# Regrouping TensorE's small products in a hybrid attention and linear-attention layer

## The chip, the cores and the metric

One core of one Trainium2 chip runs the whole layer. The metric is the device time of one execution in microseconds; less is better. The engines have short names in the profile: PE is TensorE (PEld its weight loads), DVE is VectorE, ACT is ScalarE, POOL is GpSimd and SP is SyncE, which issues most of the transfers.

## What is computed

One layer of an encoder over 512 tokens of width 2048, all in float32:

```python
h = rmsnorm(x, attn_norm_w);  proj = h @ w_in
aq, ak, av, gq, gk, gv, gr, glr = split(proj)
# group A: 16 heads x 64, three dilated windows merged by their softmax denominators
attn = mixture_of_dilations(aq, ak, av, rel_bias_table)
# group B: 4 heads, dk = 128, dv = 256, gated linear attention in both directions
o = gla_causal(q, k, v, log_a_f) + flip(gla_causal(flip(q), flip(k), flip(v), flip(log_a_b)))
gla_out = rmsnorm_per_head(o) * gla_norm_w * silu(gr)
x = x + concat(attn, gla_out) @ w_out
h = rmsnorm(x, ffn_norm_w)
x = x + (silu(h @ w_gate) * (h @ w_up)) @ w_down
out = rmsnorm(x, final_norm_w)
```

With a sequence of 512 the three windows become one dense 512x512 attention with a bias (a count of the windows that hold a key goes into it). Linear attention works in four blocks of 128 tokens: scores inside a block, masked for each direction, and a running state from block to block.

## The kernel before

The order of all instructions is written out by hand. The big matrix products are *jobs*: a job multiplies one 512-wide stretch of a weight matrix, in 16 *halves* of 12 matmuls. Each float32 operand is split into a high and a low part in a reduced format (a copy by ScalarE, L196, and a subtraction by VectorE, L197, three halves ahead), and three products of parts replace one float32 product; those are lines L285 to L287 and L293 to L295. A job holds four of the eight PSUM banks until its evacuation at the end.

Between two halves (15 times per job) `run_job` lets *side work* advance: `run_side` takes one step, up to the next `yield`, of the generator at the front of the queue `side`, after one step of an `urgent` generator if there is one. Side work has the other four PSUM banks. A slot, in PSUM or SBUF, goes back to a first-in first-out list when the program has issued its last reader. In order, the jobs are: attention's q/k and v projections (`job_qk`, `job_av`), two pairs of linear attention's q/k and v, two for the output gate (`evac_gr`, whose SiLU needs another function table on ScalarE), four for the output projection. The feed-forward part follows.

*Attention.* `attention(g)` makes one `att_step(h, b)` per yield: head h, block b of 128 queries, which is a *unit*. A step issues the unit's two score products (L553, L554). Then it transposes the softmax weights of the unit before it (`att_transpose`, four transposes, L514) and, in every second step, multiplies two units' transposed weights with v (`att_av`, eight matmuls, L522 and L523). For its own unit it reads the scores (VectorE, L566), takes the exponential (ScalarE, L584) and scales (`att_norm`, VectorE, L507 and L508). The transposed weights are split into a high part (ScalarE, L578) and a low part (VectorE, L579). `att_mix` (L532, L534) writes v's products away; after the second half of an odd head it splits the finished pair of heads (`split_of`, L355 and L356).

*Linear attention.* `gla(h)` handles one head in 17 steps. After gates and decays (ScalarE and VectorE, up to L768), the products come in these steps: for each direction the scores (L782) and the transposes of k (L786); for each direction three products for the states (L810), with scaled copies by ScalarE (L818) and sums (L820); for each pair of blocks the outputs (L841), their squares (L844) and, after one normalization (L312 to L318, L854), two groups of four transposes (L860), each followed by the scaling L863 and `gla_out`. These products are plain float32; the profile records each as two matmuls. `tables` loads a function table (L149) when another one is wanted.

Nothing in `tables`, `run_side`, `run_job` or the jobs is changed.

Of the kernel before, what the change touches and what calls it, by code (L numbers as in the profile page):

```python
# [15 lines left out]
F32 = mybir.dt.float32  # L16
F32R = mybir.dt.float32r
U32 = mybir.dt.uint32
AF = mybir.ActivationFunctionType
OP = mybir.AluOpType  # L20
# [3 lines left out]
P = 128  # L24
# [87 lines left out]
def put(*slots):  # L112
    for s in slots:
        if s.home is not None:
            s.home.free.append(s.i)


def layer(nc, tc, x, attn_norm_w, w_in, rel_table, gw_f, gb_f, gw_b, gb_b, gla_norm_w, w_out,
# [4 lines left out]
    pe, act, dve, pool, sp = nc.tensor, nc.scalar, nc.vector, nc.gpsimd, nc.sync  # L123
    mm = pe.matmul

    with tc.manual_schedule(), \
# [5 lines left out]
        s2 = Slots(p2, N2, 512, "a")  # L132
        s4 = Slots(p4, N4, 1024, "b")
# [293 lines left out]
        def load_bias(h):  # L427
            if h < NH and h not in biast:
                biast[h] = s4.get(F32, [P, BIASW])
                src = bass.AP(tensor=line.tensor, offset=line.offset + h * LINE, ap=[[1, P], [1, BIASW]])  # L430
                sp.dma_start(out=biast[h].t, in_=src)
# [65 lines left out]
                side.append(attention(2 * half))  # L497
            return f

        at = {"prev": None, "av": None, "u": 0}  # L500
        am = [small[:, 56 + i:57 + i] for i in range(4)]
        asum = [small[:, 60 + i:61 + i] for i in range(4)]
        ar = [small[:, 64 + i:65 + i] for i in range(4)]
# [6 lines left out]
        def att_transpose(u):  # L510
            h, b, n, L = u[:4]
            t = ps.get()
            for kb in range(4):
                pe.transpose(t.t[:, kb * P:(kb + 1) * P], L.t[:, kb * P:(kb + 1) * P], idn)  # L514
            put(L)
            return t
# [25 lines left out]

        def att_step(h, b):

            cur, prev, av = None, at["prev"], at["av"]
            if h is not None:
                q, k, kl = (x_[h % 2] for x_ in QK[h // 2])
                c = slice(b * P, (b + 1) * P)
                if b == 0:
                    load_bias(h)  # L550
                    load_bias(h + 1)
                s = ps.get()
                mm(s.t, q.t[:, c], k.t, start=True, stop=False)  # L553
                mm(s.t, q.t[:, c], kl.t, start=False, stop=True)  # L554
                if b == 3:
                    put(q, k, kl)
                n = at["u"]
                at["u"] += 1
            tp = att_transpose(prev) if prev else None
            if av:  # L560
                at["av"] = None
                o = att_av(*av)
            if h is not None:
                L = s2.get()
                w = biast[h].t[:, 384 - b * P:896 - b * P]
                dve.tensor_tensor_reduce(L.t, s.t, w, 1.0, 3e38, op0=OP.add, op1=OP.min,  # L566
                                         accum_out=am[n % 4])
                put(s)
                if b == 3:
                    put(biast.pop(h))  # L570
            if prev:
                ph, pb = prev[:2]
                if pb % 2 == 0:
                    at["pt"] = (s4.get(F32R, [P, 4, 256]), s4.get(F32R, [P, 4, 256]))
                pth, ptl = at["pt"]
                cc = slice((pb % 2) * P, (pb % 2 + 1) * P)
                src = tp.t.rearrange("p (k c) -> p k c", c=P)
                act.copy(pth.t[:, :, cc], src)  # L578
                dve.tensor_tensor(ptl.t[:, :, cc], src, pth.f[:, :, cc], op=OP.subtract)  # L579
                put(tp)  # L580
                if pb % 2 == 1:
                    at["av"] = (ph, pb // 2, pth, ptl)
            if h is not None:
                act.activation(L.t, L.t, AF.Exp, scale=-1.0, bias=am[n % 4], accum_out=asum[n % 4])  # L584
                cur = (h, b, n, L)
            if av:
                att_mix(av[0], av[1], o)
            if h is not None:
                att_norm(cur)
            at["prev"] = cur  # L590

        def attention(g):
            for h in range(4 * g, 4 * g + 4):
# [106 lines left out]
        def gla_out(i):  # L700
            if i in gate and i in gout:
                t, o = gate.pop(i), gout.pop(i)
                dve.tensor_tensor(o.t, o.t, t.t, op=OP.mult)
                put(t)
                mixf[8 + i] = o
                if not hT:
                    mixh[8 + i] = split_of(mixf.pop(8 + i), big=True)
# [7 lines left out]
        def gla(h):  # L715
# [26 lines left out]
            for d in range(2):  # L742
                c = fb[d]
# [19 lines left out]
                q, k = s2.get(), s2.get()  # L763
# [11 lines left out]
                put(*G["res"])  # L775

            T, kt = [], []
            for d in range(2):
                a = ps.get()
                for b in range(4):  # L780
                    c = slice(b * P, (b + 1) * P)
                    mm(a.t[:, c], ks[d].t[:, c], qs[d].t[:, c], start=True, stop=True)  # L782
                tr = ps.get()
                for b in range(4):
                    c = slice(b * P, (b + 1) * P)
                    pe.transpose(tr.t[:, c], ks[d].t[:, c], idn)  # L786
                put(ks[d])
                t = s2.get()
                pool.memset(t.t, 0.0)
                yield  # L790
                dve.copy_predicated(r3(t), masks[:, d:d + 1, :].to_broadcast([P, 4, P]),
                                    a.t.rearrange("p (b c) -> p b c", c=P))
                put(a)
                T.append(t)
                kk = s2.get()
                act.copy(kk.t, tr.t)
                put(tr)
                kt.append(kk)
            dve.tensor_tensor(T[0].t, T[0].t, T[1].t, op=OP.add)
            put(T[1])  # L800
            yield

            v = [gv[h // 2][b // 2].t[:, b % 2, (h % 2) * 256:(h % 2 + 1) * 256] for b in range(4)]
            S_ = [{}, {}]
            for d in range(2):
                order = ((0, 1, 2), (3, 2, 1))[d]
                stt = s4.get(F32, [P, 4, 256])
                us = [ps.get() for _ in range(2)]
                for n, b in enumerate(order):
                    mm(us[n // 2].t[:, (n % 2) * 256:(n % 2 + 1) * 256], kt[d].t[:, b * P:(b + 1) * P], v[b],  # L810
                       start=True, stop=True)
                put(kt[d])
                prev = None
                for n, b in enumerate(order):
                    u = us[n // 2].t[:, (n % 2) * 256:(n % 2 + 1) * 256]
                    s = stt.t[:, n]
                    fi = fs[d][:, (b if d == 0 else b - 1):(b if d == 0 else b - 1) + 1]
                    act.activation(s, u, AF.Copy, scale=fi)  # L818
                    if prev is not None:
                        dve.scalar_tensor_tensor(s, prev, fi, s, op0=OP.mult, op1=OP.add)  # L820
                    prev = s
                    S_[d][b + 1 if d == 0 else b - 1] = s
                put(*us)
                S_[d]["slots"] = stt
                yield

            on = s4.get(F32, [P, 4, 256])
            ss, rs = small[:, 76:80], small[:, 80:84]
# [2 lines left out]
            for i in range(2):  # L831
                o = ps.get()
                for b in (2 * i, 2 * i + 1):
                    c = slice(b * P, (b + 1) * P)
                    ob = o.t[:, (b % 2) * 256:(b % 2 + 1) * 256]
                    terms = [(T[0].t[:, c], v[b])]
                    for d in range(2):
                        if b in S_[d]:
                            terms.append((qs[d].t[:, c], S_[d][b]))
                    for n, (l, r) in enumerate(terms):  # L840
                        mm(ob, l, r, start=n == 0, stop=n == len(terms) - 1)  # L841
                for b in (2 * i, 2 * i + 1):
                    ob = o.t[:, (b % 2) * 256:(b % 2 + 1) * 256]
                    act.activation(junk.t[:, 0:256], ob, AF.Square, accum_out=ss[:, b:b + 1])  # L844
                os_.append(o)
                yield
            put(junk, T[0], *qs, S_[0]["slots"], S_[1]["slots"])
            if h % 2:
                put(*gv.pop(h // 2))
            rstd_of(ss, 4, rs, 1.0 / 256, (small[:, 84:88], small[:, 88:92]))  # L850
            for i in range(2):
                for b in (2 * i, 2 * i + 1):
                    c = slice((b % 2) * 256, (b % 2 + 1) * 256)
# [3 lines left out]
            for i in range(2):  # L857
                tr = ps.get()
                for b in range(4):
                    pe.transpose(tr.t[:, b * P:(b + 1) * P],  # L860
                                 on.t[:, b, i * P:(i + 1) * P], idn)
                o = s2.get()
                dve.tensor_scalar(o.t, tr.t, wcol[:, W_GLA + 2 * h + i:W_GLA + 2 * h + i + 1], None, op0=OP.mult)  # L863
                put(tr)
                gout[2 * h + i] = o
                gla_out(2 * h + i)
                yield
            put(on)


# [734 lines left out]
```

## Time and profile before

| | |
|---|---|
| median of 3 runs | 2232.04 us (2231.92 to 2236.86) |
| profiled execution | 2234.08 us, its span 2232.3 us |
| busy share of the span | TensorE 99%, VectorE 73%, ScalarE 45%, GpSimd 5% |
| linear attention's last product | 711 us |
| output projection, then feed-forward | from 681 us, from 869 us |

The span runs from the first to the last instruction of the profiled execution. The duration of a matmul's record reaches beyond the start of the next one, because matmuls are pipelined, so a row's duration is not the time that TensorE gives to it. The distance from one start to the next is.

### The profile page before, as it was taken

The page shows a single profiled execution, that of the slowest core. Times are in us where ns is not written, and L with a number is a line of the kernel's source. Part 1 is how long each engine was busy: PE and PEld are TensorE (multiplying, and loading weights), DVE is VectorE, ACT ScalarE, POOL GpSimd, SP SyncE. Part 2 cuts the span into 40 slices and gives each one's busy share as a digit, 9 for nine tenths or more (in the row PEclk, how much of TensorE's full clock was granted, in tenths as well). Part 3 has the DMA queues.
Part 4 walks back from the last instruction along what each step waited for, and adds up shares of the span by engine and source line. Part 5 has one row for each costly group of instructions (what it writes and reads, how often), then busy time and mean ns, then how long its engine had stood idle before and what let it go on. Part 6 is the DMA issues. An engine that isn't in the chain of part 4 may idle for free.

```text
span 2232.3 us, 37013 instructions
## 1 busy us (share of the span) xinstructions
PE 2207.0 (99%) x14814; PEld 2034.4 (91%) x14814; DVE 1635.4 (73%) x2717; ACT 1002.7 (45%) x1637; POOL 116.2 (5%) x173
## 2 busy tenths in 40 slices
PE   8999999999999999999999999999999999999998
PEld 6888888888888888999999999999999999999986
DVE  4366665745454436988888888888888788988877
ACT  5344454444454344444434343444334565555543
POOL 0000000000000100000000000000000110022220
PEclk9999999999999999999999999999999999999999
DMA  6525625232314332333333333333333774588992
GB/s 206 158 68 154 177 79 147 85 123 64 97 57 151 128 127 76 113 115 124 114 114 123 114 123 114 114 125 115 122 120 116 247 179 171 185 198 184 237 372 80
DMA packets 211804, 307.78 MB, mean 138 GB/s; under 512 B 15375, under 2 KB 131263, under 8 KB 211632
## 3 DMA queue, kind: packets, MB, share of 16 engines
q1 hardware_dynamic: 192480, 259.37, 36.1%
q0 software_dynamic: 18256, 44.99, 8.5%
q8 instruction: 116, 1.90, 0.3%
q10 hardware_dynamic: 896, 1.06, 0.1%
q14 instruction: 56, 0.46, 0.1%
HBM read 246.58 MB, written 46.20 MB: 131 GB/s over the span
## 4 chain that ended last, share of the span: by engine, by line
PE 94%; DVE 2%; DMA 2%; ACT 1%; issue 0%; SPq 0%; ACTq 0%; DVEq 0%
PE ps L1149 13%; PE ps L1148 13%; PE ps L1147 13%; PE ps L293 6%; PE ps L294 6%; PE ps L295 6%; PE ps L285 5%; PE ps L287 5%; PE ps L286 5%; PE ps L1376 5%; PE ps L1375 5%; PE ps L1374 5%; PE ps L514 1%; PE ps L841 1%; DMA a<-md 1%; DMA b<-gd 1%
## 5 line engine op out<-in xcount | busy, mean ns | idle before, releaser
L1149 PE MATMUL ps<-a,b 128*128 128x256 f32 x2464 | 697.7, 283 | 2.9 <-DVE b L1106 2.9
L1147 PE MATMUL ps<-a,b 128*128 128x256 f32 x2464 | 697.4, 283 | 0.0
L1148 PE MATMUL ps<-a,b 128*128 128x256 f32 x2464 | 697.3, 283 | 0.0
L1101 ACT CAST b<-b 128x768 fp32r<-128x768 f32 x480 | 445.8, 942 | 533.4 <-DVE b L1106 285.9
L1106 DVE TENSOR_TENSOR b<-b,b 128x768 fp32r<-128x768 f32 x480 | 510.3, 1089 | 132.8 <-PE ps L1148 61.8
L1149 PEld LDWEIGHTS ps<-a,b 128*128 128x128 f32 x2464 | 473.0, 192 | 3.8 <-DVE b L1106 3.8
L1148 PEld LDWEIGHTS ps<-a,b 128*128 128x128 f32 x2464 | 473.0, 192 | 0.0
L1147 PEld LDWEIGHTS ps<-a,b 128*128 128x128 f32 x2464 | 473.0, 192 | 0.0
L197 DVE TENSOR_TENSOR a<-b,a 128x512 fp32r<-128x512 f32 x292 | 195.0, 686 | 126.9 <-ACT a L196 125.7
L1376 PE MATMUL ps<-b,a 128*128 128x256 f32 x896 | 253.7, 283 | 2.7 <-DVE a L1339 2.7
L1375 PE MATMUL ps<-b,a 128*128 128x256 f32 x896 | 253.6, 283 | 0.0
L1374 PE MATMUL ps<-b,a 128*128 128x256 f32 x896 | 253.6, 283 | 0.0
L196 ACT CAST a<-b 128x512 fp32r<-128x512 f32 x292 | 171.1, 617 | 55.8 <-DMA b<-in_w_down_dram 20.9
L293 PE MATMUL ps<-a,a 128*128 128x512 f32 x464 | 183.5, 396 | 0.0
L294 PE MATMUL ps<-a,a 128*128 128x512 f32 x464 | 181.2, 391 | 2.3 <-DVE a L197 2.1
L295 PE MATMUL ps<-a,a 128*128 128x512 f32 x464 | 180.9, 390 | 0.0
L1376 PEld LDWEIGHTS ps<-b,a 128*128 128x128 f32 x896 | 172.0, 192 | 2.9 <-DVE a L1339 2.9
L1375 PEld LDWEIGHTS ps<-b,a 128*128 128x128 f32 x896 | 172.0, 192 | 0.0
L1374 PEld LDWEIGHTS ps<-b,a 128*128 128x128 f32 x896 | 172.0, 192 | 0.0
L1089 DVE TENSOR_TENSOR b<-b 128x512 f32<-128x512 f32 x240 | 164.2, 684 | 7.2 <-DMA b<-in_w_up_dram 4.3
L285 PE MATMUL ps<-a,a 128*128 128x512 f32 x416 | 168.1, 404 | 0.0
L286 PE MATMUL ps<-a,a 128*128 128x512 f32 x416 | 163.1, 392 | 0.0
(224 smaller groups left out, 3071.2 us busy)
## 6 DMA issues: line engine op xcount, KB each, us to landing
b<-in_w_gate_dram SPq DMA_DIRECT2D x88, 512.0 KB, 3.4
b<-in_w_up_dram SPq DMA_DIRECT2D x88, 512.0 KB, 3.4
b<-in_w_down_dram SPq DMA_DIRECT2D x88, 512.0 KB, 5.5
b<-in_w_in_dram SPq DMA_DIRECT2D x96, 256.0 KB, 4.5
b<-in_w_in_dram SPq DMA_DIRECT2D x48, 512.0 KB, 3.8
b<-in_w_out_dram SPq DMA_DIRECT2D x32, 512.0 KB, 4.4
md<-a POOLq DMA_DIRECT2D x56, 256.0 KB, 8.6
a<-a SPq DMA_DIRECT2D x96, 128.0 KB, 2.3
```

Of the source, the lines that this page charges most:

```text
L285: mm(o, wh.t[:, c], xh.t, start=first, stop=False)
L293: mm(o, xh.t[:, c], wh.t[:, w], start=first, stop=False)
L294: mm(o, xh.t[:, c], wl.t[:, w], start=False, stop=False)
L295: mm(o, xl.t[:, c], wh.t[:, w], start=False, stop=last)
L1101: act.copy(hi.t, src)
L1106: dve.tensor_tensor(lo.t, src, hi.f, op=OP.subtract)
L1147: mm(o, wh, xh, start=head, stop=False, skip_group_check=True)
L1148: mm(o, wh, xl, start=False, stop=False, skip_group_check=True)
L1149: mm(o, wl, xh, start=False, stop=end, skip_group_check=True)
L1374: mm(o, xh[:, t], wh, start=first and h == 0, stop=False, skip_group_check=True)
L1375: mm(o, xh[:, t], wl, start=False, stop=False, skip_group_check=True)
L1376: mm(o, xl[:, t], wh, start=False, stop=last, skip_group_check=True)
```

## The change

In attention, `att_step` collects units in `at["pair"]`. Even steps transpose both collected units one after the other (eight transposes) and split both; odd steps transpose nothing and multiply the two with v. Both transposed parts are now allotted in the even step. In linear attention the scores of both directions come first, then the transposes of k of both directions, in one step; the state products of both directions come in one step, before any of the copies, and an empty step follows; the outputs of all four blocks come in one step; the eight last transposes come in one step, with `gla_out` after both. A head has 14 steps.

```diff
-        at = {"prev": None, "av": None, "u": 0}
+        at = {"pair": [], "av": None, "u": 0}
 ...
-            cur, prev, av = None, at["prev"], at["av"]
+            av = at["av"]
+            pair = at["pair"] if h is None or b % 2 == 0 else []
 ...
-            tp = att_transpose(prev) if prev else None
+            tps = [att_transpose(u) for u in pair]
             if av:
                 at["av"] = None
                 o = att_av(*av)
 ...
-            if prev:
-                ph, pb = prev[:2]
-                if pb % 2 == 0:
-                    at["pt"] = (s4.get(F32R, [P, 4, 256]), s4.get(F32R, [P, 4, 256]))
-                pth, ptl = at["pt"]
-                cc = slice((pb % 2) * P, (pb % 2 + 1) * P)
-                src = tp.t.rearrange("p (k c) -> p k c", c=P)
-                act.copy(pth.t[:, :, cc], src)
-                dve.tensor_tensor(ptl.t[:, :, cc], src, pth.f[:, :, cc], op=OP.subtract)
-                put(tp)
-                if pb % 2 == 1:
-                    at["av"] = (ph, pb // 2, pth, ptl)
+            if pair:
+                at["pair"] = []
+                ph, pb = pair[0][:2]
+                pth, ptl = s4.get(F32R, [P, 4, 256]), s4.get(F32R, [P, 4, 256])
+                for n_, tp in enumerate(tps):
+                    cc = slice(n_ * P, (n_ + 1) * P)
+                    src = tp.t.rearrange("p (k c) -> p k c", c=P)
+                    act.copy(pth.t[:, :, cc], src)
+                    dve.tensor_tensor(ptl.t[:, :, cc], src, pth.f[:, :, cc], op=OP.subtract)
+                    put(tp)
+                at["av"] = (ph, pb // 2, pth, ptl)
 ...
-            at["prev"] = cur
+                at["pair"].append(cur)
 ...
             T, kt = [], []
+            as_, trs, ts = [], [], []
+            for d in range(2):
+                ts.append(s2.get())
+                pool.memset(ts[d].t, 0.0)
             for d in range(2):
                 a = ps.get()
                 for b in range(4):
                     c = slice(b * P, (b + 1) * P)
                     mm(a.t[:, c], ks[d].t[:, c], qs[d].t[:, c], start=True, stop=True)
+                as_.append(a)
+            for d in range(2):
                 tr = ps.get()
                 for b in range(4):
                     c = slice(b * P, (b + 1) * P)
                     pe.transpose(tr.t[:, c], ks[d].t[:, c], idn)
                 put(ks[d])
-                t = s2.get()
-                pool.memset(t.t, 0.0)
-                yield
+                trs.append(tr)
+            for d in range(2):
+                a, tr, t = as_[d], trs[d], ts[d]
                 dve.copy_predicated(...)
 ...
                 kt.append(kk)
+            yield
             dve.tensor_tensor(T[0].t, T[0].t, T[1].t, op=OP.add)
 ...
+            orders = ((0, 1, 2), (3, 2, 1))
+            uss = []
             for d in range(2):
-                order = ((0, 1, 2), (3, 2, 1))[d]
-                stt = s4.get(F32, [P, 4, 256])
                 us = [ps.get() for _ in range(2)]
-                for n, b in enumerate(order):
+                for n, b in enumerate(orders[d]):
                     mm(us[n // 2].t[...], kt[d].t[:, b * P:(b + 1) * P], v[b], start=True, stop=True)
                 put(kt[d])
+                uss.append(us)
+            for d in range(2):
+                order, us = orders[d], uss[d]
+                stt = s4.get(F32, [P, 4, 256])
                 prev = None
 ...
                 S_[d]["slots"] = stt
-                yield
+            yield
+            yield
 ...
                 os_.append(o)
-                yield
+            yield
 ...
                 gout[2 * h + i] = o
+            for i in range(2):
                 gla_out(2 * h + i)
-                yield
+            yield
             put(on)
```

## The prediction

> **What bounds the kernel now.** I read the page first (busy shares, then the chain that ended last), then the groups of TensorE's instructions kept apart by shape, then TensorE's timeline around the places that the diff touches, and last the timelines of ScalarE and VectorE around TensorE's idle places.
>
> ```profile
> core 0: 2232.3 us, clock 0.999
> ...
> PE 2207.0 (99%) x14814; PEld 2034.4 (91%) x14814; DVE 1635.4 (73%) x2717; ACT 1002.7 (45%) x1637; POOL 116.2 (5%) x173
> ...
> PE 94%; DVE 2%; DMA 2%; ACT 1%; issue 0%; SPq 0%; ACTq 0%; DVEq 0%
> ```
>
> TensorE is busy 2207.0 of 2232.3 us, at a granted clock of 0.999, and is 94% of the chain. The diff neither adds nor removes a matmul or a transpose; it only regroups them. So the change can pay or cost in two ways alone: by what it costs TensorE to turn from one kind of instruction to another, and by the few places at which TensorE waits. Busy time shows neither, because matmul records overlap. I therefore measure from start to start.
>
> The projection's weight products are the background. Fifteen of them in a row, undisturbed, lie between the rows at 128.76 and 132.16 below: 3.40/15 = 0.2267 us each, so the twelve between two steps of side work are 2.72 us. All rows are TensorE's timeline: start, duration, line, operation, tiles, count.
>
> ```profile
> 117.97 0.60 PE L514 MATMUL ps<-idn,a 128*128 128x128 f32 x4
> ...
> 121.18 0.39 PE L553 MATMUL ps<-a,a 128*128 128x512 f32 x1
> ...
> 125.31 0.60 PE L514 MATMUL ps<-idn,a 128*128 128x128 f32 x4
> ...
> 128.76 0.39 PE L285 MATMUL ps<-a,a 128*128 128x512 f32 x1
> ...
> 132.16 0.39 PE L553 MATMUL ps<-a,a 128*128 128x512 f32 x1
> ...
> 454.90 0.28 PE L522 MATMUL ps<-b,b 128*128 128x256 f32 x1
> ...
> 458.60 0.39 PE L293 MATMUL ps<-a,a 128*128 128x512 f32 x1
> ...
> 787.58 1.03 PE L347 MATMUL ps<-idn,a 128*128 128x128 f32 x8
> ...
> 791.19 0.39 PE L293 MATMUL ps<-a,a 128*128 128x512 f32 x1
> ```
>
> **Attention: transposes by eight.** Four transposes and twelve weight products take 121.18 - 117.97 = 3.21 us. The FFN's preparation already has eight transposes in a row (L347): with twelve products they take 791.19 - 787.58 = 3.61 us, though four more transposes at the pitch inside that row, (1.03 - 0.27)/7 = 0.109, would be 0.43. So doubling the group costs 0.40 and not 0.43: one group instead of two leaves 0.03 us. The rest of the pair: in an odd step the four transposes stand ahead of v's eight products; from 125.31 to 132.16, less twelve further undisturbed products (2.72), that is 4.13 us. Without transposes the same eight with twelve products take 458.60 - 454.90 = 3.70. The difference, 0.43, is the transposes' own time. A pair of steps is thus 3.21 + 4.13 = 7.34 us before and 3.61 + 3.70 = 7.31 after (scores and the further products alike in both). 32 pairs: **1.0 us gained**. Bounds: nothing, if the longer group behind two score products is dearer than the L347 row; 1.9 us, if what a lone group of four costs beyond its own time and the products (3.21 - 0.43 - 2.72 = 0.06) vanished in every pair.
>
> **Attention: the waits.** The answer for L508, which scales a unit's weights, has TensorE's loads waiting on it six times and never otherwise. The first and the last of the six steps, from score to score, with VectorE's rows ahead of the first:
>
> ```profile
>   PEld ps L514: 3.1, 6
> ...
> 158.99 0.69 DVE L356 TENSOR_TENSOR a<-a,a 128x512 fp32r<-128x512 f32 x1 [0.69 <-ACT a L355]
> ...
> 159.65 0.39 PE L553 MATMUL ps<-a,a 128*128 128x512 f32 x1
> ...
> 159.79 0.48 DVE L508 TENSOR_SCALAR a<-a,small 128x512 f32<-128x512 f32 x1
> ...
> 160.33 0.66 PE L514 MATMUL ps<-idn,a 128*128 128x128 f32 x4
> ...
> 163.57 0.39 PE L553 MATMUL ps<-a,a 128*128 128x512 f32 x1
> ...
> 426.66 0.39 PE L553 MATMUL ps<-a,a 128*128 128x512 f32 x1
> ...
> 430.58 0.39 PE L553 MATMUL ps<-a,a 128*128 128x512 f32 x1
> ```
>
> Each lasts 3.92 us. An undisturbed one is two scores (0.45) and the 3.21 above, 3.66: so 0.26 lost, 1.5 us over six. They fall where a finished head pair is split (L355, L356): the scaling of the odd step's unit stands behind it on VectorE. After the change that odd step has no PSUM copy and no subtraction for a transpose, so its exponential no longer stands behind such a copy on ScalarE (0.59 us, the first row of the next fence). I take a third of it, 0.2, an estimate, since the exponential also waits for the score's reading; the scaling then ends near 160.07 instead of 160.27, and in the following even step the four transposes of the older unit come first. TensorE, at 159.65 + 0.46 = 160.11 ready for the younger unit's now, is so again (0.43 sooner for the odd step's missing transposes, 0.43 later for the older unit's). The wait shrinks to some hundredths; I take **1.3 us gained** (bounds 0 and 1.5).
>
> What replaces it: in an even step ScalarE now makes two PSUM copies ahead of the exponential, VectorE two subtractions ahead of the scaling, and v's products wait for the second.
>
> ```profile
> 122.27 0.59 ACT L578 CAST b<-ps 128x512 fp32r<-128x512 f32 x1 [1.80 <-PE ps L514]
> ...
> 122.89 0.69 DVE L579 TENSOR_TENSOR b<-ps,b 128x512 fp32r<-128x512 f32 x1 [0.35 <-ACT b L578]
> ```
>
> The even step that begins at 121.64 with its transposes has the subtraction done at 123.58. A second one ends near 124.3. The odd step's v products would then start at 125.31 + 0.40 = 125.7 (v takes the place of that step's transposes). 1.4 us to spare, so this costs nothing; behind the two subtractions are queued the scaling (now needed two steps later) and the weights' own splitting L197, which is three halves (8 us) ahead. PSUM: a pair takes five banks over two steps out of four spare ones, in the order in which they came free; the latest reuse is of the odd step's score bank, which VectorE reads first thing and which is wanted a step later.
>
> **Linear attention.** Rows of head 0, each from the start of a group to the next one's, with twelve weight products between:
>
> ```profile
> 491.75 1.05 PE L782 MATMUL ps<-a,a 128*128 128x128 f32 x8
> 492.64 0.60 PE L786 MATMUL ps<-idn,a 128*128 128x128 f32 x4
> ...
> 495.85 1.05 PE L782 MATMUL ps<-a,a 128*128 128x128 f32 x8
> ...
> 502.67 1.46 PE L810 MATMUL ps<-b,a 128*128 128x256 f32 x6
> ...
> 506.71 1.46 PE L810 MATMUL ps<-b,a 128*128 128x256 f32 x6
> ...
> 510.75 2.32 PE L841 MATMUL ps<-b,a 128*128 128x256 f32 x10
> ...
> 515.68 0.81 PE L841 MATMUL ps<-b,a 128*128 128x256 f32 x3
> ...
> 526.05 0.60 PE L860 MATMUL ps<-idn,b 128*128 128x128 f32 x4
> ...
> 529.26 0.60 PE L860 MATMUL ps<-idn,b 128*128 128x128 f32 x4
> ```
>
> Take from each its own time (pitch in the row times count) and 2.72. Scores with transposes: 4.10 - 0.89 - 0.43 - 2.72 = 0.06. State updates: pitch (1.46 - 0.38)/5 = 0.216, six are 1.30; 4.04 - 1.30 - 2.72 = 0.02. Outputs: ten of 0.216 are 2.16; 4.93 - 2.16 - 2.72 = 0.05. Last transposes: 3.21 - 0.43 - 2.72 = 0.06. Twice each, 0.38 per head. Merged there is one of each: if a merged group turns as dearly as one old one, and the last as the L347 row (0.02), 0.15 stays. Gain 0.23, over four heads **0.9 us**. Bounds: 0.4 if only the last transposes gain (0.06 + 0.06 - 0.02 = 0.10 a head), 1.5 if all goes.
>
> New waits: the scores of direction 1 now follow at once on those of direction 0, with a step less of notice. Their operands leave VectorE well before:
>
> ```profile
> 486.74 0.68 DVE L768 TENSOR_TENSOR a<-a,a 128x512 f32<-128x512 f32 x1
> ```
>
> 487.42 against 491.75: four microseconds in hand. The six scaled copies of the states (L818) stand in one step instead of two, but two steps follow before the outputs. The memsets stay on GpSimd, which is 5% busy. No DMA moves.
>
> **Linear attention: two waits for tables.** In heads 2 and 3 the last transposes wait for the normalized outputs (L854); these are the starts of the two groups of each, and the load of the function table ahead of it on ScalarE:
>
> ```profile
> 642.87 1.28 ACT L149 ACT_TABLE_LOAD   x1
> ...
> 646.60 0.79 PE L860 MATMUL ps<-idn,b 128*128 128x128 f32 x4
> ...
> 650.01 0.60 PE L860 MATMUL ps<-idn,b 128*128 128x128 f32 x4
> ...
> 703.87 1.28 ACT L149 ACT_TABLE_LOAD   x1
> ...
> 707.07 1.31 PE L860 MATMUL ps<-idn,b 128*128 128x128 f32 x4
> ...
> 710.97 0.60 PE L860 MATMUL ps<-idn,b 128*128 128x128 f32 x4
> ```
>
> 3.41 and 3.90 against 3.21: 0.20 and 0.69 lost. The generator `gla` has 17 yields per head before and 14 after, and a job takes 15 side steps. Before, two heads (34) run over the 30 steps of the second q/k and v jobs, so heads 2 and 3 meet `evac_gr`'s SiLU table in mid-head and load the other table back right ahead of L854. After, 28 steps fit in 30; head 2 starts with the first gate job and ends inside it, head 3 ends inside the second. Both loads leave the path: **0.9 us gained** (bounds 0 and 0.9). Head 3 now loads its table in its second step, some seven halves (19 us) ahead of its first products; what is late next there has room.
>
> **Sum.** 1.0 + 1.3 + 0.9 + 0.9 = 4.1 us. The profiled execution took 2234.08 us, 1.8 more than its span, and would take 2230.0; the median of the runs is 2232.04, so 2227.9. 0.3% is 6.7 us, about what a measurement of this kernel can tell from no change. The upper bounds together, 1.9 + 1.5 + 1.5 + 0.9 = 5.8, do not reach it.
>
> **The rivals.** *The waits stay.* The younger unit's scaling still comes late for the second four transposes, and merged groups turn as dearly as two. Then 1.0 of the transposes and 0.4 of the last ones are left: 2230.6. For it: the margin at 160.1 is a few hundredths. Against: the odd step loses work on both engines. Within 0.3%.
>
> *Slower: v's products wait for the second low half.* VectorE works in program order, so if it is 1.4 us behind in an even step, every odd step's v products stop TensorE. To come out slower by over 0.3% it has to eat 4.1 + 6.7 = 10.8 us, 0.34 us in each of the 32; then 2238.8. For it: VectorE gets 0.7 us more in even steps. Against: the second low half has two such subtractions to spare, and only the steps near a job's evacuation are fuller.
>
> *Slower: the clock.* The eight transposes that follow sixteen score records could lower TensorE's clock; twelve products at half rate would cost 2.7 us more, and over 4 heads 10.9 us: 2238.8 as well. The eight in a row at 787.58 are followed by products at the full rate (3.61 in all), which leaves this little. [...]
>
> *Faster by over 0.3%.* All turning gone and some stall at a later stage's start with it: 2225 or less. Nothing in the rows names such a stall.
>
> **How the numbers follow.** Forecast 0.65, the first rival 0.19, the slower ones 0.07 and 0.02, the faster one 0.07. Faster 0.07, same 0.84, slower 0.09. The range goes from all upper bounds (2232.0 - 5.8 = 2226.2) less 0.5 for the scatter of a median, 2225.7, to 0.7 over the first rival, 2231.3, which leaves out the slower ones.
>
> **What would show it.** Groups of eight at L514, 32 of them, and 3.61 us from such a group to the end of its twelve products; no wait of L514 on L508; v's products first in odd steps at 3.70; one group each per head at L782, L810, L841, L860; the last linear-attention transposes before 690 us instead of 711, and one table load fewer. It is wrong if TensorE idles ahead of L522, or a merged group costs more than two did.

## The result, and the profile after

| | before | after |
|---|---|---|
| median of 21 runs each | 2234.92 us (2231.92 to 2237.4) | 2230.86 us (2227.45 to 2232.62) |
| profiled execution | 2234.08 us, span 2232.3 | 2230.84 us, span 2229.1 |
| from the transposes behind the first 24 weight products to the first feed-forward product | 850.84 us | 846.86 us |

The ratio is 0.9984, 95% interval 0.9978 to 0.9990: 2.2 to 4.9 us faster. The medians lie 4.06 us apart, and the forecast was 4.1. Single executions scatter more than that, by 5.5 us before and 5.2 after; the last section shows why.

The page after. Instruction counts of the compute engines are the same; TensorE's share of the chain rises from 94% to 97%.

```profile
span 2229.1 us, 37003 instructions
...
PE 2206.0 (99%) x14814; PEld 2039.6 (92%) x14814; DVE 1627.6 (73%) x2717; ACT 1002.5 (45%) x1637; POOL 115.7 (5%) x173
...
PE 97%; DMA 1%; DVE 1%; ACT 0%; issue 0%; SPq 0%; ACTq 0%; DVEq 0%
```

Where the time went is seen with a ruler laid over both traces. The first 24 weight products are left off, since some of them run slowly and their number differs from execution to execution (the last section). The ruler goes from the transposes behind them to the first feed-forward product. TensorE's timeline of before:

```profile
18.30 0.60 PE L335 MATMUL ps<-idn,a 128*128 128x128 f32 x4
...
869.14 0.28 PE L1147 MATMUL ps<-a,b 128*128 128x256 f32 x1
```

and of after:

```profile
16.86 0.60 PE L335 MATMUL ps<-idn,a 128*128 128x128 f32 x4
...
292.42 1.03 PE L514 MATMUL ps<-idn,a 128*128 128x128 f32 x8
...
296.02 0.39 PE L555 MATMUL ps<-a,a 128*128 128x512 f32 x1
...
597.35 1.95 PE L787 MATMUL ps<-a,a 128*128 128x128 f32 x16
599.13 1.04 PE L793 MATMUL ps<-idn,a 128*128 128x128 f32 x8
...
605.46 2.75 PE L818 MATMUL ps<-b,a 128*128 128x256 f32 x12
...
613.54 4.48 PE L854 MATMUL ps<-b,a 128*128 128x256 f32 x20
...
623.35 1.03 PE L873 MATMUL ps<-idn,b 128*128 128x128 f32 x8
...
626.96 0.63 PE L724 MATMUL ps<-a,a 96*128 96x512 f32 x2
...
863.72 0.28 PE L1161 MATMUL ps<-a,b 128*128 128x256 f32 x1
```

869.14 - 18.30 = 850.84 and 863.72 - 16.86 = 846.86: 3.98 us gone there. (The profiled executions differ by 3.2 in all: the one of after began the ruler 1.44 us sooner and took 2.16 us longer behind it, on identical code.) Eight of attention's transposes with twelve products take 296.02 - 292.42 = 3.60 us. In linear attention the first three groups of a head are each followed by 24 products (5.44), because the step between them gives TensorE nothing to do: 8.11, 8.08 and 9.81 us from start to start; less their own times (1.78 + 0.87, 2.59, 4.31) and 5.44 they cost 0.02, 0.05 and 0.06 for turning. The last group, with twelve products, takes 3.61. The last transposes of all begin at 675.24 us; they were forecast before 690.

The last transposes of linear attention (now L873) no longer wait for anything. Of the six waits on L508 the answer for that line shows two. It leaves out short ones, though, as an even step after a split pair of heads shows (VectorE's rows of the same stretch among TensorE's):

```profile
  PEld ps L514: 0.3, 2
```

```profile
157.15 0.69 DVE L356 TENSOR_TENSOR a<-a,a 128x512 fp32r<-128x512 f32 x1 [0.69 <-ACT a L355]
...
157.56 0.39 PE L555 MATMUL ps<-a,a 128*128 128x512 f32 x1
...
157.95 0.49 DVE L508 TENSOR_SCALAR a<-a,small 128x512 f32<-128x512 f32 x1
...
158.02 1.13 PE L514 MATMUL ps<-idn,a 128*128 128x128 f32 x8
...
161.74 0.39 PE L555 MATMUL ps<-a,a 128*128 128x512 f32 x1
```

From score to score that step is 161.74 - 157.56 = 4.18 us. Undisturbed, such a step takes 4.07 (a row of one stands with the run that splits later). The group of eight lasts 1.13 instead of 1.03; 0.11 us is still waited, and 0.84 in the six steps together.

### The profile page after: what moved, and what is told of

It is laid out like the page before. It is cut to its first block, busy times and chain, and to the rows that moved or that the text cites. A ratio compares the mean times of both kernels' runs of the same rounds, so it can differ in the third digit from the quotient of the medians.

```text
span 2229.1 us, 37003 instructions
## 1 busy us (share of the span) xinstructions
PE 2206.0 (99%) x14814; PEld 2039.6 (92%) x14814; DVE 1627.6 (73%) x2717; ACT 1002.5 (45%) x1637; POOL 115.7 (5%) x173
## 4 chain that ended last, share of the span: by engine, by line
PE 97%; DMA 1%; DVE 1%; ACT 0%; issue 0%; SPq 0%; ACTq 0%; DVEq 0%
PE ps L1163 13%; PE ps L1162 13%; PE ps L1161 13%; PE ps L294 6%; PE ps L293 6%; PE ps L295 6%; PE ps L285 5%; PE ps L286 5%; PE ps L287 5%; PE ps L1390 5%; PE ps L1389 5%; PE ps L1388 5%; PE ps L514 1%; PE ps L854 1%; DMA a<-md 1%; PE ps L523 1%
## 5 line engine op out<-in xcount | busy, mean ns | idle before, releaser
L1390 PE MATMUL ps<-b,a 128*128 128x256 f32 x896 | 254.8, 284 | 2.7 <-DVE a L1353 2.7
L196 ACT CAST a<-b 128x512 fp32r<-128x512 f32 x292 | 170.4, 618 | 49.8 <-DMA b<-in_w_down_dram 22.8
L1390 PEld LDWEIGHTS ps<-b,a 128*128 128x128 f32 x896 | 172.9, 193 | 2.9 <-DVE a L1353 2.9
```

The lines of the kernel that those rows point to most:

```text
L1390: mm(o, xl[:, t], wh, start=False, stop=last, skip_group_check=True)
```

## The experiments

Each is one edit of the kernel before or after. The ruler is the one above, from two rows of each trace; the times come from 11 runs of each (21 of the changed kernel); for the last row and for one experiment without a row there is a single execution, the profiled one. The expectations count from the first weight product, so of their figures the differences are to be compared.

| | ruler us | against | ratio of times to before |
|---|---|---|---|
| before | 850.84 | | |
| after | 846.86 | -3.98 to before | 0.9984 (0.9978 to 0.9990) |
| attention only | 848.56 | -2.28 to before | 0.9992 (0.9983 to 1.0001) |
| linear attention only | 849.05 | -1.79 to before | 1.0001 (0.9992 to 1.0009) |
| after, 3 empty steps | 849.35 | +2.49 to after | 0.9996 (0.9987 to 1.0005) |
| after, split later | 845.97 | -0.89 to after | 0.9986 (0.9977 to 0.9995) |
| before, split later | 849.13 | -1.71 to before | 0.9993 (0.9984 to 1.0002) |
| after, v in even steps | 845.60 | -1.26 to after | 0.9981 (0.9973 to 0.9990) |
| after, scores between | 847.93 | +1.07 to after | |

A change of one or two microseconds is at the edge of what eleven runs tell. The ruler, on code that waits little, tells about a tenth: attention's groups of four, the same in the kernel before and in the one with linear attention alone changed, cost 3.5 us above their own time in both traces. The granted clock is 1.00 over the whole ruler in the traces of before and after.

**Attention only.** `att_step` and its dictionary from the change, `gla` as before.

> Only the attention part of the change; linear attention as before. Measured on TensorE from the first weight product to the first feed-forward product: 858.4 us before, 854.3 after. Theory (turning between kinds of instructions, plus waits): attention brings 2.1 of the 4.1 us (1.1 turning, 0.9 waits for the scaled weights, 0.1 elsewhere), so 856.3, with the eight waits of linear attention's last transposes unchanged (0.2 and 0.7 us) and the table load ahead of them still there. Rival (the gain comes from linear attention's fewer side steps, attention's regrouping only moves work): 858.4, no change of the stretch. Time: 2.1 us less than before by the theory, ratio 0.9991.

2.28 less where 2.1 was expected. The two groups that wait behind table loads take 3.41 and 3.90 us to the next one, as before. The rival falls: attention's regrouping alone moves TensorE.

**Linear attention only.** `gla` from the change, the rest as before.

> Only the linear attention part; attention as before. Theory: 0.9 us of turning (scores and transposes 0.34, last transposes 0.38, outputs 0.18, state products nothing) and 0.9 us of the two waits behind table loads, so the stretch from the first weight product to the first feed-forward product is 856.6 us, with attention's six waits unchanged at about 0.25 us each. Rival (its gain is only the two table loads): 857.5. Time: 1.8 us less than before, ratio 0.9992.

1.79 less where 1.8 was expected, and the sum with the first part, 4.07, is the whole change's 3.98 within a tenth. The rival's 0.9 is excluded by the ruler. The time does not show it: the ratio is 1.0001, with 0.9992 at the interval's end, though the plain medians of the same session, 2233.77 and 2235.18, lie 1.4 us apart. The last section shows a scatter large enough to cover 1.8 us.

**Three empty steps.**

```diff
             yield
             put(on)
+            yield
+            yield
+            yield
```

> The changed kernel with three empty side steps at the end of each head of linear attention, so a head has 17 steps as before. Theory (the two waits went because the heads no longer straddle the loads of the other function table): the table loads stand ahead of the last transposes of heads 2 and 3 again, and the waits of about 0.2 and 0.7 us come back: stretch 855.2 us against 854.3. Rival (the waits went because the outputs are made together and their squares start sooner): 854.3, no waits.

Both waits are back, behind the same table loads as before. ScalarE's timeline, then TensorE's:

```profile
633.74 1.28 ACT L149 ACT_TABLE_LOAD   x1
...
694.49 1.28 ACT L149 ACT_TABLE_LOAD   x1
```

```profile
637.47 1.22 PE L873 MATMUL ps<-idn,b 128*128 128x128 f32 x8
...
697.70 1.74 PE L873 MATMUL ps<-idn,b 128*128 128x128 f32 x8
...
704.51 0.39 PE L295 MATMUL ps<-a,a 128*128 128x512 f32 x1
705.58 0.50 PE L293 MATMUL ps<-a,a 128*128 128x512 f32 x1 [0.69 <-ACT a L196]
```

The groups of eight last 1.22 and 1.74 us instead of 1.03: 0.19 + 0.71 = 0.90, as the theory has it. The ruler shows 1.6 more than that. Most of it nobody expected: head 3 now ends inside the output projection, where `gla_out` splits both results at once, and a weight half's copy (L196) is queued behind them on ScalarE; the first of the stops, at 704.51, is 0.84 us by itself. It takes both splits at once: in the kernel before, head 3 also ends inside the output projection (711 us, which begins at 681), but its two splits stand a step apart and TensorE does not stop behind them (busy for all of the 9.00 us from 711 on). So ending earlier is no part of the change's gain; it only keeps a cost away that the merged last step would have brought.

**The split later**, in the changed kernel:

```diff
-            if hf == 1 and h % 2 == 1:
-                mixh[pr] = split_of(mixf.pop(pr))
+            return pr if hf == 1 and h % 2 == 1 else None
 ...
                 att_norm(cur)
                 at["pair"].append(cur)
+            if av and done is not None:
+                mixh[done] = split_of(mixf.pop(done))
```

> The changed kernel, with the splitting of a finished pair of heads put behind the scaling of the step's own unit instead of ahead of it. Theory (the rest of attention's waits, 0.85 us over six steps, is the scaling standing behind that split on VectorE): the six groups of eight transposes that cost 138 to 218 ns above their own time cost 25 ns like the others; stretch 853.4 us against 854.3, time 0.9 less than the changed kernel. Rival (the scaling is late by its own chain of exponential and sum): they stay, 854.3.

The step that corresponds to the one above, and what VectorE does in it:

```profile
158.04 0.39 PE L554 MATMUL ps<-a,a 128*128 128x512 f32 x1
...
158.50 1.03 PE L514 MATMUL ps<-idn,a 128*128 128x128 f32 x8
...
162.11 0.39 PE L554 MATMUL ps<-a,a 128*128 128x512 f32 x1
```

```profile
157.63 0.69 DVE L356 TENSOR_TENSOR a<-a,a 128x512 fp32r<-128x512 f32 x1
158.24 0.68 DVE L197 TENSOR_TENSOR a<-b,a 128x512 fp32r<-128x512 f32 x1
```

L356 now has the scaling ahead of it, the group is 1.03, the step 4.07 against 4.18. All six waits are gone, 0.89 us. The rival, a chain that is late by itself, falls.

**The split later, in the kernel before:** the same edit.

> The kernel before, with one edit: a finished pair of heads is split behind the scaling of the step's own unit instead of ahead of it. Theory (attention's waits are that order on VectorE, and have nothing to do with how transposes are grouped): the six steps with 299 to 399 ns above their own time fall to 59 like the other 26, so 1.7 us less, stretch from the first weight product to the first feed-forward product 856.7 us against 858.4; time 1.7 less than before. Rival (they need the regrouping, because the older unit's transposes have to come first): they stay, 858.4.

1.71 less on the ruler; the time, 0.9993, is not clear of no change. So attention's six waits were one matter, the order of two things on VectorE, and the regrouping another. The change did half of the first by the way: 1.7 of waiting before, 0.9 after.

**More transposes.** The list of the younger unit's transposes is repeated, so that heads 0 to 3, 4 to 7, 8 to 11 and 12 to 15 have groups of 8, 12, 16 and 20:

```diff
-            for kb in range(4):
+            for kb in list(range(4)) * (1 + (h // 4 if b % 2 else 0)):
```

> The changed kernel with the younger unit's four transposes repeated into the same bank: not at all in heads 0 to 3, once in heads 4 to 7, twice in 8 to 11, three times in 12 to 15, so groups of 8, 12, 16 and 20. Their own time at 0.1085 us each is taken off. Theory (a turn costs TensorE a fixed amount whatever the size of the group, and it is smaller for groups over four): 25 ns for all four sizes. Rival (the cost goes up and down with the number of instructions in the group, as the state products' 27 for six and 54 for twelve hint): 25 at 8, near 59 at 12, 25 or 29 at 16, near 59 at 20.

Rows of 12, 16 and 20, from score to score with twelve products:

```profile
262.34 0.39 PE L555 MATMUL ps<-a,a 128*128 128x512 f32 x1
...
262.79 1.47 PE L514 MATMUL ps<-idn,a 128*128 128x128 f32 x12
...
266.88 0.39 PE L555 MATMUL ps<-a,a 128*128 128x512 f32 x1
...
341.66 0.39 PE L555 MATMUL ps<-a,a 128*128 128x512 f32 x1
...
342.12 1.91 PE L514 MATMUL ps<-idn,a 128*128 128x128 f32 x16
...
346.60 0.39 PE L555 MATMUL ps<-a,a 128*128 128x512 f32 x1
...
429.68 0.39 PE L555 MATMUL ps<-a,a 128*128 128x512 f32 x1
...
430.14 2.34 PE L514 MATMUL ps<-idn,a 128*128 128x128 f32 x20
...
435.10 0.39 PE L555 MATMUL ps<-a,a 128*128 128x512 f32 x1
```

4.54, 4.94 and 5.42 us. Take off the scores and products (0.45 + 2.72) and 0.1085 per transpose: 0.07, 0.03 and 0.08. With the 0.06 of four and the 0.02 to 0.03 of eight this alternates: the rival was right, and the theory of a fixed cost per turn falls. Groups of 8 and 16 cost 0.02 to 0.03 us here, those of 4, 12 and 20 cost 0.06 to 0.08. Why is not settled, nor why twelve records of state products cost twice what six do (0.05 and 0.02). What the prediction used, the row of eight at L347, was a lucky size.

**Scores between** the two units' transposes in even steps, so they come as four, two scores, four.

> The changed kernel with the older unit's four transposes ahead of the even step's two score products and the younger unit's behind them. Nothing else moves, and the younger unit has as much notice as before. Theory (each return from transposes to the long products costs, and a group of four costs more than one of eight): an even step costs 59 ns above its own time or more, against 25, 1.0 us more over 30 steps. Rival (only the last group before a long stretch of products counts, and it counts by the sum of transposes): 25.

1.07 more over 30 steps, 0.036 each, where 1.0 was expected. The agreement is partly luck: step by step, an undisturbed even step turns for 0.066 instead of 0.025 us, which is more than 1.07 in all, while the six waits became 0.4 us shorter. Separating the transposes costs even with only two products between. Whether that is because two groups are left or because the last one is of four (0.06 by itself) the run does not tell.

**v's products in even steps,** behind the eight transposes; odd steps issue scores alone:

```diff
-            av = at["av"]
+            av = at["av"] if h is None or b % 2 == 0 else None
```

> The changed kernel with the products with v of the pair before moved from the odd step into the even step, right behind its eight transposes, so odd steps issue scores alone. Theory (what counts is how often TensorE comes back from a group to the long products): the even step costs 20 ns above its own time as transposes with v's products did before (19), the odd step nothing, against 25 and 20: 0.7 us less over 30 pairs. The mixing and the splitting move to even steps too, where the unit just scaled is needed two steps later, so the six remaining waits (0.85 us) go. Stretch 852.7 us against 854.3, time 1.6 less than the changed kernel. Rival (VectorE and ScalarE have too much in even steps: two copies, two subtractions, mixing and scaling): v's products or the next even step's transposes wait, and the stretch is 854.3 or more.

```profile
298.50 0.39 PE L555 MATMUL ps<-a,a 128*128 128x512 f32 x1
...
298.95 1.03 PE L514 MATMUL ps<-idn,a 128*128 128x128 f32 x8
299.75 0.36 PE L522 MATMUL ps<-b,b 128*128 128x256 f32 x1
...
303.53 0.39 PE L555 MATMUL ps<-a,a 128*128 128x512 f32 x1
```

1.26 less than after where 1.6 was expected: the waits went (0.9), and of 0.7 for turning half came. An even step is 5.03 us; less 0.45, 0.87, 0.95 for v's products (eight of 0.119) and 2.72 it turns for 0.04. The 0.02 expected is not by the same time per product; at 0.119 the step of before, four transposes with v's products, turns for 4.13 - 0.43 - 0.95 - 2.72 = 0.03. This version beats the kernel before in time (0.9981) and the changed one on the ruler; in time it cannot be told from the changed one.

## Why the prediction was right or wrong

**Right: the mechanism and the sum.** TensorE's work is unchanged, and what moved is turning and waiting. 4.1 was forecast; the ruler shows 3.98. That the medians show 4.06 is in part luck, since their interval leaves 2.2 to 4.9.

**Wrong, and the step that failed: the bound for no change.** The prediction took 0.3%, 6.7 us, for what a measurement of this kernel can tell from no change, without saying from which runs, and put 0.84 of the chance there. The measured 0.16% lies inside it, but with an interval of 0.06% to either side it is clearly told from no change. What spreads by 0.25% (2231.92 to 2237.4) is a single execution; the ratio of two sets of 21 is known to 0.06%. The forecast, 0.18% faster by its own sum, ought to have been called a gain.

**Wrong: the base.** The time, 2227.9, is 3.0 too low. It was taken from the median of three runs, 2232.04, and 21 runs of the same kernel have 2234.92: two of those three lay at the low end. The sentence that carries 4.1 from the profiled execution to that median failed. The profiled execution, 2234.08, would have given 2230.0, within 0.9 of what was measured, but by luck: it is one execution out of the same scatter. Among the experiments' eleven runs the profiled one was the slowest of its kernel once (linear attention only) and the fastest once (v in even steps).

Term by term:

- Attention's turning: 1.0 forecast. Summed over all its steps, start to start less own times, it fell from 2.5 us to 1.4: 1.1. The step was sized rightly (3.60 for 3.61), with luck in it: the L347 row that it was taken from has eight transposes, one of the cheap sizes.
- Attention's waits: 1.3 forecast, 0.9 came. The term's own bound, 1.5, was too low as well: it took the first and the last of the six steps for all, and the six cost 1.7. The scaling did end in time by the forecast's own reckoning: at 157.95 + 0.49 = 158.44, with the younger unit's turn at 158.02 + 4 x 0.1085 = 158.45. Still the group took 0.10 us longer. The step left out that a transpose's operand is loaded into TensorE ahead of the product. In an undisturbed step the load of the fifth transpose starts at 150.13 and its product at 150.24; here the load starts at 158.49, behind the scaling's end, and the product at 158.50. So here the scaling had to be done about a tenth before the turn, the 0.11 us between that load and its product (no run moved the load alone). A row of the prediction already showed the tenth: there the scaling ended at 160.27, the group began at 160.33 and lasted 0.66 instead of 0.60. The first rival was partly right.
- Linear attention's turning: 0.9 forecast. Last transposes, 0.09 a head, and scores, also 0.09, did better than one group's price; the state products gained nothing, the outputs 0.04. Four heads: 0.9. The sum was right by two errors that cancel.
- Table waits: 0.9 forecast and had, by the mechanism named, as the empty steps show. But no load was saved: the loads are seven in both traces. The two that stood ahead of last transposes (642.87 and 703.87) now come at 632.27, behind those of head 2, and at 865.39, where TensorE waits for neither.
- Slower rivals: v's products waited nowhere, even with mixing and splitting added to the even step. Nor did the clock fall behind sixteen records of scores and eight transposes (0.02 us of turning at 597.35, granted clock 1.00). For groups of up to twenty in a row no run here shows a loss by it: the step with twenty turned for 0.08 us, where twelve products at half rate would cost 2.7.

## What to carry to other kernels

On an engine that is busy all the time, measure small groups from start to start, in a row of the trace that already has the size to be built, and take the time of the whole, and what can be told from no change, from more runs than three; a profiled execution is one run like any other. Look for what a waiting instruction is queued behind: moving one split behind one scaling gave 1.7 us on the ruler without any regrouping. When steps of side work get fewer, see which stage their ends now fall into.

## What the runs showed that was not expected

The scatter of the times has a cause that is seen: spells of 3.41 us with TensorE's granted clock at 0.50 after a stop, in some executions and not in others. After the same stop near the end, of 2.46 us from start to start before and 2.39 after (2.07 and 2.00 idle), the granted clock (the sixth figure behind the stretch's length) is, in the changed kernel, then in the kernel before:

```profile
2145.60:2149.20 3.60, 3.60 (x11) 2.79 (x10) 3.60 (x6) 0.00 (x1) 0.63 (x2) 0.53 1.06 341
```

```profile
2149.00:2152.60 3.60, 3.60 (x17) 2.96 (x16) 3.60 (x7) 0.34 (x1) 1.05 (x2) 1.00 1.08 313
```

11 products run where 17 did. In the attention-only kernel it came after a stop of 1.42 us idle at the feed-forward's start:

```profile
894.90:898.30 3.40, 3.40 (x18) 3.40 (x17) 3.34 (x5) 1.12 (x2) 0.00 (x0) 0.50 0.00 0
```

The feed-forward's products start 0.213 us apart there and 0.12 apart ahead of it, so a spell filled with them costs about 1.5 us (an estimate: the 16 products that 3.41 us hold at 0.213, at 0.093 each). Behind the same stop of 1.42 us the clock stays at 1.00 in the kernel before and in the changed one. The longest stop has spells too: 2.67 us idle ahead of a product of L1390 (L1376 in the kernel before). Around its end the clock is 0.50 for 3.41 us in the changed kernel's trace, while it stays at 1.00 in that of the kernel before.

Behind the ruler, on identical code, the kernel before takes 1363.2 us without a spell and the changed one 1365.3 with two (the stretch at 0.50 behind TensorE's last product, which both traces have, is left out). The mean clock of each execution goes with its time in the same way. Of the 33 executions of the kernel before that belong to the first experiments, ten have 0.999 and take 2231.47 to 2233.69 us, five have 0.998 and take 2234.16 to 2235.41, eighteen have 0.997 and take 2234.49 to 2236.64. The kernel with linear attention alone changed has six at 0.998, 2232.14 to 2233.77 us, and five at 0.997, 2234.65 to 2236.16, the profiled one among these: the scatter is larger than the 1.8 us of its ruler. Whether its eleven runs had more spells than the kernel before, no trace shows.

What decides whether a stop brings a spell is not shown either. A stop of 2.67 us idle brought one in one trace and none in another; one of 2.00 was followed by a spell, one of 2.07 by none, and one of 1.42 by a spell in one trace of three.

At the start, the first weight products are slow: seven in the kernel before, six in the changed one and twelve in the one with empty steps start 0.42 to 0.58 us ahead of the next instruction, most of them 0.43, where the later ones stand 0.23 apart.
